# Gate products from two operands, stabiliser rows through memory, and fewer state steps in a one-core encoder layer

## The chip, the cores and the metric

The kernel runs on one core of one Trainium2 chip. The metric is the time of one execution on the device in microseconds (us); lower is better. A core has five engines that matter here: TensorE (PE in the profile, with its weight loads as PEld), VectorE (DVE), ScalarE (ACT), GpSimd (POOL) and SyncE (SP), which only issues DMA transfers in this kernel. Each engine works through its own instructions in the order in which they were written; semaphores hold an instruction back until its inputs are there.

## The reference: what is computed

One encoder layer on x of 2048 tokens by 1024 channels, in float32, between two RMS norms. One input projection gives the operands of two mixers that work side by side: chunked band attention (8 heads of 64) and an mLSTM recurrence (4 heads of 128). Their outputs are gated, summed, projected and added to x; then comes a feed-forward block of width 4096 with a squared ReLU.

The part that the change touches is the recurrence. In the reference:

```python
ig, logf = i_pre, log_sigmoid(f_pre)          # one value per token and head
bcum = cumsum(logf)
dmat = bcum[t] - bcum[s] + ig[s]              # for s <= t, else -inf
m_t  = maximum(bcum + m_state, max_s dmat)    # the stabiliser
dw   = exp(dmat - m_t)
qk   = (q @ k.T) * dw
num  = exp(bcum + m_state - m_t) * (C_state @ q) + qk @ v
den  = exp(bcum + m_state - m_t) * (n_state @ q) + sum(qk)
out  = num / maximum(abs(den), exp(-m_t))
```

The state C, n, m starts at zero and is carried from one chunk of tokens to the next. `i_pre` and `f_pre` are eight columns of the input projection, xn @ w_in: the gates.

## The kernel before

**Blocks.** The 2048 tokens are four blocks (0 to 3) of T = 512, each cut into NT = 4 steps of 128 tokens. A float32 product is made of three single-pass products of split operands: every operand is kept as a high part (rounded, dtype fp32r) and a low part (the rest), and high x high, high x low, low x high are summed (`mm3` at L548 and the loops in `quad`, L597, and `product`, L626). A weight tile of 128x1024 is fetched into one of four `wraw` buffers, then ScalarE rounds it (L489) and VectorE forms its low part (L491) in one of three `wsp` buffers; it serves 24 matmuls.

**Strassen's form.** The large products are run by a two-by-two block scheme with seven products instead of eight. The operand for product m is `A[m][k]`. For the input projection the two rows of blocks are two token blocks, the two columns are the two halves of the 1024 channels: A[0] = a11, A[1] = a12, A[2] = a21 + a22, A[5] = a11 - a21, A[6] = a22, where a11 and a12 are the halves of the first token block (0 or 2), a21 and a22 those of the second (1 or 3).

**The order of the work.** Nothing here is a plain loop. Python generators ("threads", `Flow` at L104) yield requests: `("pe", ns)`, `("act", ns)`, `("dve", ns)`, `("pool", ns)` or `("sp", ns, latency)` with a planned duration, `wait` for events, `get` for buffers. `Flow.run` always takes the request that can start first by these planned times and emits its instructions at once. So the order of each engine's instructions in the program follows from planned durations; on the chip the order is fixed and only the semaphores hold. A changed duration or a dropped instruction places all that comes behind it anew. The dense products (`dense`, L836) form one thread of the lowest rank; all others are put between them.

**Stages.** First the projections of v for blocks 0 and 1 (`token_tiles`), then the input projection of blocks 0 and 1 (`quad`), then that of blocks 2 and 3 (`in_far`, L661) with the mixers of blocks 0 and 1 beside it; then the output projection, the up projection and the down projection (`down`) for blocks 0 and 1, the mixers of blocks 2 and 3 lying beside the last up and the down projection; then the same for blocks 2 and 3, and the final norm. `project(b)` (L920) multiplies the mixers' outputs of block b with their weights; its merges are at L960. It waits until all of them are there (`mixed`).

**The gates.** `gate_mm` (L1373) multiplies the 40 columns of `gw` (eight gate columns, zeros, eight low parts) with `A[m][k]`, eight matmuls of 512 columns a call and pair (m, k0), at L1378. `gates` (L1333) brings the 40 rows to VectorE and transposes them. Block 0: (0,0) and (1,4). Block 1: (0,0), (6,4), and in a second bank (5,0), which is subtracted at L1348. Blocks 2 and 3 share the (0,0) product in `in_far`: it is copied out after the second input group and stored in memory (`gates_kept`, L1366), then (1,4) is added in the same bank for block 2; much later (6,4) and (5,0) follow for block 3, and the stored part is added.

**The stabiliser rows and the head.** `gates_rest` (L1392) turns the gates of a block into all per-token factors; at its end four transposes (L1478) put the stabiliser m_t of the four heads into rows of a bank, and ScalarE (L1480) and VectorE (L1483) keep high and low part in `mtt`. `recurrence` (L1487) runs the four heads of a block one after the other (one place in `rec_room`). Per head, `load_rec` (L1500) writes a column of ones (L1505, GpSimd) and fetches keys, queries (L1509) and values. `rec_head` (L1524) builds exp(dmat - m_t): two matmuls of 512 columns into one bank, the first (L1532) with the causal mask, 0 or -1e30, from bf16 tiles, the second (L1533) with minus m_t of this head copied to all partitions, both over all four steps; four exponentials on ScalarE read the bank (L1537). Then keys are transposed (L1544) and scaled (L1548), k times q is formed (L1555), and each of the four steps has three fp32 products of 129 columns, which take two passes each: with the weights (L1569), the state's update (L1570) and the old state times q (L1571). VectorE updates the state (L1574); `rec_out` (L1622) sums. GpSimd has one power per head (L1591). The recurrence of block b waits for that of block b - 1.

**The norms.** `norm_in` (L976) and `stats_far` (L1003) form 1/sqrt(mean) by a power on GpSimd (L1001, L1023), planned at 960 ns; `rows_far` (L1026) spreads the result by matmuls (L1036). `norm_mid` (L2000) sums squares over partitions with one fp32 matmul of 512 columns against ones (L2012).

## Time and profile before

| what | value |
|---|---|
| median of 3 runs | 2765.6 us (2764.7 to 2769.62) |
| the profiled execution | 2766.63 us |
| its span, first to last instruction | 2764.9 us |
| mean granted TensorE clock | 0.999 |
| DMA moved | 679.28 MB, 246 GB/s in the mean |

The profile is one execution taken by the hardware profiler. Its page gives the busy time of each engine, slices of the span, DMA queues, the chain of work that ended last, and the costliest groups of instructions by line. A group's line reads: line, engine, operation, output<-inputs, shapes, count, then busy time and mean length of one, then idle time of the engine just ahead of them and who ended it. Matmuls overlap in their pipeline, so their lengths add up to more than the time that they take; the distance of their starts is what counts. In the list of waits a row reads: who waited <- for whom, then us in total, times, longest.

### The profile page before, as it was taken

The numbers are of one execution on the slowest core, as the hardware profiler recorded it, in microseconds if no ns is written. First come the engines' busy times: TensorE is split into PE (matmuls) and PEld (weight loads), VectorE is DVE, ScalarE is ACT, GpSimd is POOL, SyncE is SP. The second block draws the span as 40 slices with busy tenths as digits, with TensorE's granted clock in tenths as the row PEclk, the third lists the DMA queues.
The fourth block names the chain that finished last, engine by engine and source line by source line (L and its number), as shares of the span: only waits on it lengthen the run. The fifth ranks groups of instructions, "written<-read, shape, count | busy, mean of one in ns | idle before, by whom it ended". The sixth has DMA issues, their size and how long they took to land.

```text
span 2764.9 us, 38314 instructions
## 1 busy us (share of the span) xinstructions
PE 2733.3 (99%) x12916; PEld 2268.9 (82%) x12916; DVE 2098.3 (76%) x3719; ACT 1552.8 (56%) x2667; POOL 42.2 (2%) x108
## 2 busy tenths in 40 slices
PE   9999999999999999999999999999999999999998
PEld 7878888888888878888888888888888888888887
DVE  7868776787986678997667888788888665667675
ACT  6545456766763435566456776566445555554543
POOL 0000000000000000000000000000000000000000
PEclk9999999999999999999999999999999999999999
DMA  8877678878988899767769876777765464578863
GB/s 280 294 249 269 235 252 268 249 249 274 291 267 271 302 304 313 265 210 264 255 232 295 245 234 213 247 228 226 260 232 172 151 218 152 182 260 279 285 237 115
DMA packets 329704, 679.28 MB, mean 246 GB/s; under 512 B 36692, under 2 KB 62164, under 8 KB 329508
## 3 DMA queue, kind: packets, MB, share of 16 engines
q1 hardware_dynamic: 329364, 676.83, 73.1%
q8 instruction: 101, 1.65, 0.2%
q14 instruction: 95, 0.78, 0.1%
q10 hardware_dynamic: 144, 0.01, 0.0%
HBM read 465.07 MB, written 211.63 MB: 245 GB/s over the span
## 4 chain that ended last, share of the span: by engine, by line
PE 82%; DVE 8%; DMA 3%; issue 3%; ACT 3%; POOL 1%; SPq 0%; POOLq 0%; ACTq 0%; DVEq 0%
PE bank L619 35%; PE bank L551 9%; PE bank L550 9%; PE bank L552 9%; PE bank L650 9%; PE bank L655 2%; PE bank L1216 2%; PE bank L1323 2%; DVE wsp L491 2%; PE bank L1292 2%; DVE r L1080 1%; DMA ctx<-in_xt 1%; DVE sc L1298 1%; ACT wsp L489 1%; PE bank L1378 1%
## 5 line engine op out<-in xcount | busy, mean ns | idle before, releaser
L619 PE MATMUL bank<-r,wsp 128*128 128x512 f32 x4872 | 1113.2, 390 | 3.2 <-DVE ctx L1749 1.6
L619 PEld LDWEIGHTS bank<-r,wsp 128*128 128x128 f32 x4872 | 912.7, 188 | 197.6 <-DVE ctx L1749 2.5
L489 ACT CAST wsp<-wraw 128x1024 fp32r<-128x1024 f32 x453 | 475.7, 1050 | 492.5 <-PE bank L551 172.2
L491 DVE TENSOR_TENSOR wsp<-wraw,wsp 128x1024 fp32r<-128x1024 f32 x453 | 552.7, 1220 | 235.8 <-ACT wsp L489 222.7
L550 PE MATMUL bank<-r,wsp 128*128 128x512 f32 x1152 | 454.5, 395 | 0.0
L551 PE MATMUL bank<-r,wsp 128*128 128x512 f32 x1152 | 449.4, 390 | 0.0
L552 PE MATMUL bank<-r,wsp 128*128 128x512 f32 x1152 | 449.4, 390 | 0.0
L650 PE MATMUL bank<-r,wsp 128*128 128x512 f32 x1512 | 370.7, 393 | 0.8 <-DVE r L1328 0.6
L650 PEld LDWEIGHTS bank<-r,wsp 128*128 128x128 f32 x1512 | 277.5, 188 | 55.0 <-DVE r L1328 1.1
L552 PEld LDWEIGHTS bank<-r,wsp 128*128 128x128 f32 x1152 | 216.3, 188 | 45.9
L551 PEld LDWEIGHTS bank<-r,wsp 128*128 128x128 f32 x1152 | 216.6, 188 | 40.7
L550 PEld LDWEIGHTS bank<-r,wsp 128*128 128x128 f32 x1152 | 216.4, 188 | 40.6
L1080 DVE TENSOR_TENSOR r<-r 128x512 fp32r<-128x512 f32 x271 | 180.3, 686 | 52.5 <-ACT r L1075 51.0
L1075 ACT CAST r<-r 128x512 fp32r<-128x512 f32 x271 | 163.3, 622 | 92.1 <-DMA r<-u 72.6
L1749 DVE TENSOR_TENSOR ctx<-bank,ctx 128x512 f32<-128x512 f32 x150 | 102.5, 685 | 63.3 <-PE bank L619 63.1
L508 DVE TENSOR_TENSOR wraw<-wraw,wraw 128x1024 f32<-128x1024 f32 x112 | 136.2, 1218 | 2.5 <-DMA wsum<-wraw 1.4
L1304 ACT ACTIVATE sc<-sc,scs 128x640 f32<-128x640 f32 (+4 forms) x128 | 97.4, 761 | 50.4 <-DVE scs L1298 49.9
L2067 ACT ACTIVATE ctx<-ctx 128x512 f32<-128x512 f32 x96 | 60.5, 631 | 102.8 <-DVE ctx L1749 102.5
L1741 ACT COPY ctx<-bank 128x512 f32<-128x512 f32 x150 | 87.1, 581 | 50.9 <-PE bank L619 49.9
L1328 DVE TENSOR_TENSOR r<-bank,r 128x512 fp32r<-128x512 f32 (+1 forms) x168 | 96.1, 593 | 16.2 <-ACT r L1326 15.6
L1216 PE MATMUL bank<-r,r 128*128 128x512 f32 x336 | 95.7, 367 | 2.2 <-DVE r L1328 2.2
L1326 ACT CAST r<-bank 128x512 fp32r<-128x512 f32 (+1 forms) x168 | 80.4, 516 | 21.1 <-PE bank L1323 19.6
(248 smaller groups left out, 3014.3 us busy)
## 6 DMA issues: line engine op xcount, KB each, us to landing
wraw<-in_wf SPq DMA_DIRECT2D x202, 512.0 KB, 4.3
wraw<-wsum SPq DMA_DIRECT2D x120, 512.0 KB, 4.8
r<-u SPq DMA_DIRECT2D x224, 256.0 KB, 4.4
u<-ctx SPq DMA_DIRECT2D x128, 256.0 KB, 2.2
u<-tmp SPq DMA_DIRECT2D x96, 256.0 KB, 2.3
wraw<-in_w SPq DMA_DIRECT2D x47, 512.0 KB, 4.2
ctx<-in_wf SPq DMA_DIRECT2D x88, 256.0 KB, 4.0
wsum<-ctx SPq DMA_DIRECT2D x88, 256.0 KB, 3.3
```

Source lines behind the costliest of these rows:

```text
L489: nc.scalar.copy(w[:, 0], raw)
L491: nc.vector.tensor_sub(w[:, 1], raw, w[:, 0].bitcast(F32))
L508: V.tensor_sub(dst, x, y)
L550: mm(ps, lh, rh, start=first, stop=False)
L551: mm(ps, lh, rl, start=False, stop=False)
L552: mm(ps, ll, rh, start=False, stop=last)
L619: mm(ps, wv[:, x, k, n], a[:, y], start=new and k == 0 and x == y == 0, stop=k == 3 and x == 1, skip_group_check=True)
L650: mm(ps, wv[:, x, k, n], a[:, y], start=start and x == y == 0, stop=stop and x == 1, skip_group_check=True)
L1075: self.nc.scalar.copy(dst[:, 0], src)
L1080: self.nc.vector.tensor_sub(dst[:, 1], src, dst[:, 0].bitcast(F32))
L1216: nc.tensor.matmul(bkv[:, :, c0:c0 + w], st, sl[:, :, o:o + w], start=n == 0, stop=n == total - 1)
L1749: nc.vector.tensor_add(t[:, o:o + 512], ps, t[:, o:o + 512])
```

## The change

The change has five parts.

1. **Gates of the second blocks.** `gw` gets four more column groups, the difference of the gate weights of the second and the first half of the channels. Block 1 is then (2,0) and (6,8) in one bank: (a21 + a22) with the first half's weights plus a22 with the difference. Block 2 is (0,0) and (1,4) in one go. For block 3, (2,0) is stored by `gates_kept` when its operand is there, and (6,8) is added to it later. The subtraction L1348, its bank and the event `gclear` go.
2. **Stabiliser rows.** `gates_rest` copies the four rows to a buffer and stores them in memory. `load_rec` fetches one row per head with a load that repeats it on all 128 partitions, into the buffer of the weights, `w`, ahead of keys, queries and values; GpSimd then sets the entries outside the causal triangle to 1e30 in place (`affine_select`, 128x512). The exponentials read `w` with scale -1. The two matmuls L1532 and L1533, the tiles `identb`, `maskb`, `sel`, `nsel`, `mtt` and L1483 go.
3. **Empty state steps.** In block 0, step 0 the product with the old state (which is zero) and its addition are left out. In block 3, step 3 the key's transpose, its scaling and the state's update, which nobody reads, are left out.
4. **The sum in `norm_mid`.** The row of sums is split into high and low part; two single-pass matmuls against ones take the place of the fp32 one. ScalarE's copy and VectorE's subtraction are new.
5. **Planned durations.** The power on GpSimd is planned at 2400 ns in `norm_in` and 5000 in `stats_far`, 960 before. The `temp` buffers are 512 wide, 516 before.

```diff
@@ setup_late
+        nc.vector.tensor_sub(raw[:, 64:96], raw[:, 32:64], raw[:, 0:32])
...
@@ in_far
                     if i == 1:
-                        (gbk,) = yield "get", self.banks, 1
-                        yield from self.gate_mm(gbk, A, ((0, 0),), True, False)
-                        fl.spawn(self.gates_kept(gbk, gclear), 1)
-                    if i == 2:
-                        yield "wait", [gclear]
-                        yield from self.gate_mm(gbk, A, ((1, 4),), False, True)
-                        fl.spawn(self.gates(2, gbk), 1)
+                        (bk,) = yield "get", self.banks, 1
+                        yield from self.gate_mm(bk, A, ((0, 0), (1, 4)), True, True)
+                        fl.spawn(self.gates(2, bk), 1)
...
-                if g == 2 and i == 1:
-                    (one, two) = yield "get", self.banks, 2
-                    yield from self.gate_mm(one, A, ((6, 4),), True, True)
-                    yield from self.gate_mm(two, A, ((5, 0),), True, True)
-                    fl.spawn(self.gates(3, one, two, True), 1)
+                if i == 1:
+                    (bk,) = yield "get", self.banks, 1
+                    yield from self.gate_mm(bk, A, ((2, 0),) if g == 1 else ((6, 8),), True, True)
+                    fl.spawn(self.gates_kept(bk) if g == 1 else self.gates(3, bk, True), 1)
@@ norm_in, stats_far
-        yield "pool", 960
+        yield "pool", 2400
...
-            yield "pool", 960
+            yield "pool", 5000
@@ gates_in
-        for b, use in ((0, (((0, 0), (1, 4)),)), (1, (((0, 0), (6, 4)), ((5, 0),)))):
+        for b, use in ((0, ((0, 0), (1, 4))), (1, ((2, 0), (6, 8)))):
...
@@ gates_rest
-        nc.scalar.copy(self.mtt[:MH], bk[:MH])
-        yield "dve", dve_ns(512)
-        yield "dve", 85
-        V.tensor_sub(self.mtt[32:32 + MH], bk[:MH], self.mtt[:MH].bitcast(F32))
+        nc.scalar.copy(tmp[:MH, :512], bk[:MH])
         fl.put(self.banks, bk)
         fl.set(B["gates"])
+        fl.spawn(self.store(self.mtd.ap()[b], tmp[:MH, :512], B["rows"], self.temp, tmp), 1)
@@ load_rec
         nc.gpsimd.memset(mvv[:, :, 128:129], 1.0)
+        yield "wait", [B["rows"]]
+        yield "sp", 800, 2000
+        nc.sync.dma_start(w[:, :512], self.mtd.ap()[b, h:h + 1].to_broadcast([P, T]))
+        yield "pool", 1000
+        nc.gpsimd.affine_select(out=w[:, :512], in_=w[:, :512], pattern=[[0, NT], [1, P]], compare_op=ALU.is_ge,
+                                fill=-NEG, base=0, channel_multiplier=-1)
+        fl.set(B["row_ev"][h])
         for to, x in ((k, MH + h), (q, h)):
@@ rec_head
-        yield "wait", [B["gates"]]
-        (bk,) = yield "get", self.banks, 1
-        yield "pe", 440
-        mm(bk.rearrange("p (c t) -> p c t", c=NT), self.identb, self.maskb.to_broadcast([P, NT, P]), start=True, stop=False)
-        mm(bk, self.nsel[:, h:h + 1].to_broadcast([P, P]), self.mtt, start=False, stop=True)
+        yield "wait", [B["gates"], B["row_ev"][h]]
...
-            nc.scalar.activation(w[:, c * P:(c + 1) * P], bk[:, c * P:(c + 1) * P], AF.Exp,
+            nc.scalar.activation(w[:, c * P:(c + 1) * P], w[:, c * P:(c + 1) * P], AF.Exp, scale=-1.0,
                                  bias=self.sm["u"][:, n:n + 1])
...
+        kept = NT - 1 if b == NB - 1 else NT
...
+            old = b > 0 or c > 0
...
             mm(bk[:, 0:129], w[:, sl], mv[c], start=True, stop=True)
-            mm(bk[:, 130:259], kt[:, sl], mv[c], start=True, stop=True)
-            mm(bk[:, 260:389], q[:, sl], cst, start=True, stop=True)
+            if c < kept:
+                mm(bk[:, 130:259], kt[:, sl], mv[c], start=True, stop=True)
+            if old:
+                mm(bk[:, 260:389], q[:, sl], cst, start=True, stop=True)
@@ norm_mid
+        nc.scalar.copy(self.part, tot[:, :512])
...
-        nc.tensor.matmul(bk, self.ones[:, 0:1].to_broadcast([P, P]), tot[:, :512], start=True, stop=True)
+        for x in range(2):
+            yield "pe", 227
+            nc.tensor.matmul(bk, self.onesr[:, 0:1].to_broadcast([P, P]), self.part, start=x == 0, stop=x == 1,
+                             skip_group_check=True)
+            if x == 0:
+                yield "dve", dve_ns(512)
+                nc.vector.tensor_sub(self.part, tot[:, :512], self.part.bitcast(F32))
```

89 lines of the change are left out of this document (36 added, 53 removed).

## The prediction

> **What bounds the kernel now.** I read the page's busy line and slices first, then the stages, then the timeline of TensorE.
>
> ```profile
> span 2764.9 us, 38314 instructions
> PE 2733.3 (99%) x12916; PEld 2268.9 (82%) x12916; DVE 2098.3 (76%) x3719; ACT 1552.8 (56%) x2667; POOL 42.2 (2%) x108
> PE   9999999999999999999999999999999999999998
> PEclk9999999999999999999999999999999999999999
> PE 82%; DVE 8%; DMA 3%; issue 3%; ACT 3%; POOL 1%; SPq 0%; POOLq 0%; ACTq 0%; DVEq 0%
> ```
>
> TensorE is busy in 99% of the span, at full clock, in every slice, and holds 82% of the chain of work that ended last. Busy alone proves little, since matmuls overlap; the spacing of their starts decides. From the timeline of TensorE:
>
> ```profile
> 447.62 2.88 PE L619 MATMUL bank<-r,wsp 128*128 128x512 f32 x12
> 450.34 0.39 PE L1532 MATMUL bank<-maskb,identb 128*128 128x512 bf16 x1
> 450.38 0.58 PE L1533 MATMUL bank<-mtt,nsel 128*128 128x512 f32 x1
> 450.80 4.94 PE L619 MATMUL bank<-r,wsp 128*128 128x512 f32 x21
> 455.58 0.60 PE L1544 MATMUL bank<-const,r 128*128 128x128 f32 x4
> 455.94 3.70 PE L619 MATMUL bank<-r,wsp 128*128 128x512 f32 x15
> 459.47 1.05 PE L1555 MATMUL bank<-r 128*128 128x128 f32 x8
> ```
>
> The columns are start, length from first start to last end, line, shapes, count. 21 matmuls of 512 columns take 4.94 us, the last one 0.39 of it, so starts are (4.94 - 0.39)/20 = 0.227 us apart. That is the slot of one matmul, whatever its own 0.39 us says: the queue is full and each slot that goes shortens the stream by 0.227 us. The stages show where this holds (columns: stage, its length, then busy time and count of TensorE, weight loads, DVE, ACT, POOL):
>
> ```profile
> 60.00:400.00 340.00, 337.63 (x1502) 274.88 (x1501) 266.75 (x414) 168.75 (x262) 5.97 (x6) 1.00 0.73 259
> 500.00:600.00 100.00, 96.48 (x532) 80.80 (x532) 79.12 (x235) 68.06 (x163) 5.50 (x17) 1.00 0.74 229
> 700.00:800.00 100.00, 98.52 (x540) 84.04 (x540) 88.07 (x213) 70.71 (x150) 3.25 (x11) 1.00 0.88 281
> 1700.00:1800.00 100.00, 97.97 (x532) 82.78 (x531) 76.65 (x180) 58.17 (x134) 3.72 (x8) 1.00 0.77 239
> 1900.00:2700.00 800.00, 799.17 (x3577) 661.81 (x3576) 578.03 (x795) 424.49 (x632) 3.23 (x4) 1.00 0.64 221
> ```
>
> Even where the mixers (attention and recurrence) run beside the dense products, TensorE is idle only 1.5 to 3.5 us in 100. So the end is set by the sum of TensorE's slots, plus about 30 us of gaps.
>
> **The change, part by part.** First what TensorE loses.
>
> ```profile
> L1378 PE MATMUL bank<-r,gw 128*40 128x512 f32 x72 | 18.1, 395 | 0.0
> L1532 PE MATMUL bank<-maskb,identb 128*128 128x512 bf16 x16 | 6.2, 389 | 0.0
> 464.46 0.39 PE L1569 MATMUL bank<-ctx,ctx 128*128 128x129 f32 x2
> 464.69 0.39 PE L1570 MATMUL bank<-ctx,ctx 128*128 128x129 f32 x2
> 464.91 0.39 PE L1571 MATMUL bank<-cst,r 128*128 128x129 f32 x2
> 465.05 1.64 PE L650 MATMUL bank<-r,wsp 128*128 128x512 f32 x6
> 466.52 0.39 PE L1569 MATMUL bank<-ctx,ctx 128*128 128x129 f32 x2
> 1300.86 1.02 PE L2012 MATMUL bank<-bias,ones 128*128 128x512 f32 x2
> 1301.32 4.92 PE L619 MATMUL bank<-r,wsp 128*128 128x512 f32 x19
> ```
>
> 1. Gates. Block 1 took 24 matmuls, with the difference weights 16; blocks 2 and 3 together take 32 before (8 for a product that both use, 8 more for block 2, 16 more for block 3) and 32 after (16 and 8 + 8). 72 become 64: 8 x 0.227 = 1.8 us.
> 2. Mask and stabiliser row. 16 heads lose the pair L1532 and L1533; the pair stands between starts at 450.34 and 450.80, that is 0.46 us: 16 x 0.46 = 7.3 us.
> 3. Empty state. A step of the recurrence has three fp32 products (two passes each). From 464.46 to 466.52 are 2.06 us with six slots of L650 (1.36), so the three cost 0.70, one 0.233 us. In block 0, step 0, four heads leave out the product with the state: 4 x 0.233 = 0.9 us. In block 3, step 3, four heads leave out the state update, 0.233, and one transpose: from 455.58 to 459.47 are 3.89 us with fifteen slots (3.40), so four transposes cost 0.48, one 0.12. 4 x 0.353 = 1.4 us.
> 4. The row sum in norm_mid. One fp32 product becomes two single-pass products. The nineteen L619 behind it end their last start 5.22 us after 1300.86 (1301.32 + 4.92 - 0.39 + 0.227 - 1300.86 = 5.22), of which 19 x 0.227 = 4.31 are theirs: the old one costs 0.91, the new two 0.45. 4 x 0.45 = 1.8 us.
>
> Sum: 1.8 + 7.3 + 0.9 + 1.4 + 1.8 = **13.2 us** of TensorE's stream.
>
> Second, the planner's allowance for the power on GpSimd rises from 960 ns to 2400 (norm_in) and 5000 (stats_far). The trace shows why it matters:
>
> ```profile
> PE bank L1036 <- POOL r_in L1001: 2.5, 2, 1.2
> PE bank L1036 <- POOL r_in L1023: 1.8, 1, 1.8
> 197.05 1.01 POOL L1023 TENSOR_TENSOR r_in<-r_in,half 128x4 f32<-128x4 f32 x1 [145.72 <-DVE r_in L1021]
> 249.70 4.38 POOL L1023 TENSOR_TENSOR r_in<-r_in,half 128x4 f32<-128x4 f32 x1 [51.65 <-DVE r_in L1021]
> 49.39 1.94 POOL L1001 TENSOR_TENSOR r_in<-r_in,half 128x4 f32<-128x4 f32 x1 [18.63 <-DVE r_in L997]
> 71.01 6.06 DMA ctx<-in_xt
> 249.54 0.74 DVE L1656 SCALAR_TENSOR_TENSOR tmp<-tmp,gcol,bias 128x512 f32<-128x512 f32 x1
> 252.00 1.22 DVE L491 TENSOR_TENSOR wsp<-wraw,wsp 128x1024 fp32r<-128x1024 f32 x1
> ```
>
> TensorE idles 4.3 us in all because L1036 was placed before GpSimd was done. A later place lets other products go first. I count the 1.8 us (the stage at 250 is dense) and not the 2.5: the later of those two powers starts at 49.39, and up to 77 us the chain of work that ended last still runs over loads of x, so products moved forward there would only wait for those. Bounds 0 and 4.3. Total **15 us**.
>
> Third, what is added and what hides it. Per block the rows are stored (one issue) and per head fetched by a 256 KB broadcast load; SP issues 20 more. In this trace such loads land in 4.1 us (r<-mfar), and SP already stands in line without TensorE feeling it:
>
> ```profile
> r<-mfar SPq DMA_DIRECT2D x32, 256.0 KB, 4.1
> SPq L451 <- DVE wsp L491: 299.3, 152, 8.1
> ```
>
> The new row load waits on SP until the store has landed, some 4 us, in front of weight loads and u loads; single waits of up to 8.1 us stand in that queue now (152 of them for L451), covered by the four raw weight tiles, one per 24 slots or 5.4 us. I cost it at nothing; without that cover it is 4 x 4 = 16 us. For the first head the keys and queries are now issued behind the row, not ahead of it.
>
> The masked select on GpSimd over 128x512 has no row in this trace. From below: a memset of 64 columns takes 146 ns and one of 4 takes 109, which is 0.6 ns a column and 0.42 us for 512. From above: 4.4 us, the longest GpSimd row. I take 1.0 us, the usual power row, the nearest one that reads SBUF. The Trainium skill, "GPSIMD Engine Reference", section 3.1, has about 1.8 cycles per element for a tight loop and about 12 with data-dependent branching; at its 1.2 GHz that is an estimate of 0.8 or 5.1 us, and no run here shows either. By the first the sum stays at 15 us; by the second the blocking described below would cost 16 x 5.1 / 2 = 41 us and the time be 2792.
>
> So per head row load plus select, 4.1 + 1.0, stand ahead of the exponentials, and in each block the store some 4 more. Keys are issued about 4 us later than now. Behind the waiting select on GpSimd stand only bias memsets and the power of the head before; behind the exponentials on ACT stand the casts of weights. The block grows by about 9 + 4 x 3 = 21 us. What waits for it is the projection:
>
> ```profile
> 1667.98 0.69 DVE L1607 TENSOR_TENSOR ctx<-bank,tmp 128x512 f32<-128x512 f32 x1
> 1724.35 0.68 DVE L960 SCALAR_TENSOR_TENSOR tmp<-tmp,bank 128x512 f32<-128x512 f32 x1
> ```
>
> Block 2, the tightest, ends its recurrence at 1668.7 and its projection first merges at 1724.35: 56 us of cover for 21. Past 56 each microsecond would count fully.
>
> ACT and DVE gain a little: four L1483 (0.68), two L1348 (0.67) and eight small ones go, four splits in norm_mid come (0.69 on DVE, 0.62 on ACT); they are off the path by the stages above, and I cost them at nothing.
>
> The profiled execution took 2766.63 us around its span of 2764.9; the median is 2765.6. 15 off the median gives **2751 us**.
>
> **The rivals.**
>
> A wait takes the removed slots' place. ACT is in order, and the plan allows 3.8 us for row load and select where I expect 5.1.
>
> ```profile
> ACT r L1075 <- DMA r<-u: 72.6, 73, 4.2
> ACT ctx L1537 <- PE bank L1533: 10.2, 5, 5.5
> ```
>
> ACT now waits about 1 us at each late u load, and it once waited 5.5 us at the exponentials, without a gap of that size on TensorE. For it: ACT is 58 to 71% busy there, and the casts feed TensorE. Against it: three split weight tiles are 16 us of cover. If TensorE loses 0.5 us per head, 16 x 0.5 = 8 are given back: 2759.
>
> GpSimd and DVE block each other; this one ends slower. The power at 249.70 took 4.38 us while DVE ran two-input operations without a pause from 249.54 to 253.2, and 1.01 us beside an idle DVE at 197.05: the two exclude each other, and the select reads 128 times as many columns. If it takes 4.4 us and holds DVE for it, DVE loses 16 x 4.4 = 70 us in the mixer stages, where it is 77 to 88% busy and makes the low halves of the weights (L491). Two selects per 100 us are 8.8 us; at 700 to 800 only 12 are free. It decides from about 6 us a select in the mean, or earlier where two fall behind one another; with half of the 70 landing on TensorE the time is 2751 + 35 = 2786. Against it: in this trace it is GpSimd that waits, DVE's lengths stay as they are (1.22 at 252.00).
> The Trainium skill, "SBUF — State Buffer", section "Who interferes with whom", says that a DVE instruction with two SBUF inputs and a GpSimd instruction that reads SBUF share a read interface, and whichever starts first blocks the other for its whole length. The trace agrees for GpSimd behind DVE (4.38 against 1.01); DVE behind GpSimd isn't shown in it.
>
> The change gives more: all of the 4.3 us, and a new order closes a few of the 15 us of gaps in the mixer stages: 2745.
>
> The rebuilt order loses what the slots give. The planner places every instruction anew, and gaps of 1 to 2 us appear elsewhere; eight of 1.5 us make 2763. That the slots don't go at all is excluded: their instructions are gone.
>
> **How the numbers follow.** Forecast 0.62 (2746 to 2757); wait in the removed slots' place 0.15 (2759, 2756 to 2763); order loses it 0.06 (2763); more 0.07 (2745); blocking 0.10 (2786). About 0.2% (5.5 us) is what a measurement of this kernel can tell from no change, so faster means under 2760.1 and slower over 2771.1. Faster: 0.62 + 0.07 + two thirds of 0.15 + 0.02 = 0.81. Slower: 0.10. Same: 0.09. The range reaches from the better case to the order's loss, 2743 to 2763; outside are the blocking and a tenth.
>
> **What would show it.** TensorE's matmul count falls by 8 for the gates, 32 for mask and row, 8 and 12 for the empty steps (two passes a product, one a transpose), and 0 in norm_mid, 60 in all, and its busy time by about 13 us, at idle near 30. The select's row gives its length, and beside it L491's mean tells whether DVE was held (1220 ns now). The waits of ACT's exponentials on GpSimd tell the first rival: over 30 us in all would bear it out. L1036 should wait for GpSimd no more. The prediction is wrong if idle of TensorE in 400 to 900 and 1480 to 1900 grows by more than 5 us.

## The result and the profile after

The kernel after takes 2759.52 us (median of 8 runs, 2756.09 to 2762.49), the kernel before, beside it on the same chip, 2766.97 us (8 runs, 2761.78 to 2772.07). The ratio is 0.9973, 95% interval 0.9962 to 0.9984: 7.5 us faster, where the sum said 15. The direction was right, the size about half. The page of the kernel after, its profiled execution taking 2758.38 us:

```profile
span 2756.6 us, 38227 instructions
...
PE 2725.7 (99%) x12856; PEld 2265.7 (82%) x12856; DVE 2098.2 (76%) x3715; ACT 1551.2 (56%) x2665; POOL 50.4 (2%) x124
```

TensorE has 60 instructions fewer, as forecast, but its busy time fell by 7.6 us, not by 13, and its idle time stayed (2756.6 - 2725.7 = 30.9 against 31.6). So 5.6 us of the forecast loss of busy time are missing. Three stretches of 3.41 us each, in which TensorE was granted half its clock, hold 5.1 of them, since work at half clock counts as busy (see Theory C). The same stages as before the change, and one more (1100 to 1200), with the columns of the prediction; the number after the five engines is the granted clock:

```profile
60.00:400.00 340.00, 339.99 (x1515) 278.14 (x1515) 265.56 (x410) 171.38 (x265) 3.73 (x8) 1.00 0.75 265
500.00:600.00 100.00, 95.44 (x521) 79.16 (x520) 80.06 (x225) 69.46 (x166) 6.92 (x17) 1.00 0.82 249
700.00:800.00 100.00, 97.96 (x538) 82.96 (x537) 81.23 (x202) 69.36 (x156) 4.69 (x14) 0.98 0.88 289
1100.00:1200.00 100.00, 98.16 (x424) 80.02 (x423) 91.40 (x125) 57.03 (x85) 0.00 (x0) 0.98 0.64 220
1700.00:1800.00 100.00, 97.40 (x506) 81.94 (x507) 76.24 (x193) 54.07 (x117) 4.65 (x10) 0.98 0.75 240
1900.00:2700.00 800.00, 797.27 (x3571) 660.23 (x3570) 578.50 (x805) 425.59 (x637) 3.23 (x4) 1.00 0.63 219
```

The first stage lost its gap (337.63 busy before, 339.99 now: the wait of the row spread is gone). Three stages show a clock of 0.98, which the profile before never had there. What the prediction named as its tests, first the groups by line of GpSimd, of ScalarE and of VectorE:

```profile
L1488 POOL TENSOR_SCALAR_AFFINE_SELECT ctx<-ctx 128x512 f32<-128x512 f32 x16 | 11.4, 713 | 103.7 <-DMA ctx<-mrow 103.3 <-ACT ctx L1529 0.3
```

```profile
L1518 ACT ACTIVATE ctx<-ctx,g_u 128x128 f32<-128x128 f32 x64 | 22.2, 394 | 3.3 <-POOL ctx L1488 3.3
```

```profile
L482 DVE TENSOR_TENSOR wsp<-wraw,wsp 128x1024 fp32r<-128x1024 f32 x453 | 553.4, 1222 | 223.6 <-ACT wsp L480 215.4
```

Then the row's load in the list of transfers (count, KB each, us from issue to landing; 4.1 was assumed), and TensorE's longest rows in the list of waits:

```profile
ctx<-mrow SPq DMA_DIRECT2D x16, 256.0 KB, 5.3
```

```profile
PE bank L1308 <- ACT sc L1296: 4.1, 4, 2.6
PE bank L1277 <- DVE scs L1283: 3.0, 3, 1.2
PE bank L1201 <- DVE r L1313: 2.5, 2, 1.3
PE bank L1021 <- POOL r_in L986: 1.5, 2, 1.0
```

The select takes 0.71 us (1.0 was assumed, between 0.42 and 4.4). The exponentials wait 3.3 us in all for it; over 30 would have borne out the first rival. VectorE's low halves take 1222 ns where they took 1220, 0.9 us more over all 453, so the second rival's blocking isn't there to speak of. The row spread (L1021 now) still waits 1.5 us, of 4.3. The first three waits of TensorE stood in the profile before too, at 2.5, 0.3 and 2.2 us, and have grown. All three end links of the attention: its transposes (L1308) wait for the softmax's normalisation (L1296), its scores (L1277) for the row minima that free the banks (L1283), its products (L1201) for the split transposes (L1313).

**Where along the kernel.** The dense matmuls are 10560 in every kernel here. The start of the k-th in one trace less that in another tells how much has been gained up to there. Worked out from the traces, in us, each column what was gained or lost within a stretch (the stretch between 302 and 393 changes nothing):

```
stretch, starts in before (us)      5-302  393-898   898-1454  1454-1980  1980-2752   sum
dense matmuls                      0-1200 1600-3200 3200-5600  5600-7200  7200-10559
beside them                               mixers0,1           mixers2,3
due by the prediction                -3.6     -2.8      -2.7      -5.1       -0.9   -15.1
after less before                    -6.4     +1.0      +0.4      -1.9       -1.5    -8.4
```

(Due in the second stretch: eight pairs 3.65 and four empty steps 0.93 go, eight gate slots of the moved (2,0) come.) The start gave more than was due (2.4 of its 6.4 us by 123 us, where profiles of the same order differ by about 2); both mixer stages, and the dense stretch between them, gave little or nothing: 3.8, 3.1 and 3.2 us less than was due. In each of these three stands one place with new waits of TensorE, 1.8 to 2.6 us, and 3.41 us at half clock behind them (at 750, 1128 and 1701 us; shown under Theory C).

### The profile page after: what moved, and what is told of

It reads as the page before. It is cut to its first block, busy times and chain, and to the rows that moved or that the text cites. A ratio compares the mean times of both kernels' runs of the same rounds, so it can differ in the third digit from the quotient of the medians.

```text
span 2756.6 us, 38227 instructions
## 1 busy us (share of the span) xinstructions
PE 2725.7 (99%) x12856; PEld 2265.7 (82%) x12856; DVE 2098.2 (76%) x3715; ACT 1551.2 (56%) x2665; POOL 50.4 (2%) x124
## 3 DMA queue, kind: packets, MB, share of 16 engines
q8 instruction: 101, 1.65, 0.2%
## 4 chain that ended last, share of the span: by engine, by line
PE 88%; DVE 5%; issue 2%; ACT 2%; DMA 2%; POOL 0%; SPq 0%; POOLq 0%; ACTq 0%; DVEq 0%
PE bank L610 38%; PE bank L541 10%; PE bank L542 10%; PE bank L543 10%; PE bank L641 10%; PE bank L646 2%; PE bank L1201 2%; PE bank L1277 2%; PE bank L1308 2%; DVE wsp L482 1%; ACT wsp L480 1%; PE bank L1551 0%; ACT sc L1289 0%; DVE r L1065 0%; DMA r<-qfar 0%
## 5 line engine op out<-in xcount | busy, mean ns | idle before, releaser
L482 DVE TENSOR_TENSOR wsp<-wraw,wsp 128x1024 fp32r<-128x1024 f32 x453 | 553.4, 1222 | 223.6 <-ACT wsp L480 215.4
L1313 DVE TENSOR_TENSOR r<-bank,r 128x512 fp32r<-128x512 f32 (+1 forms) x168 | 96.5, 593 | 10.2 <-ACT r L1311 9.3
L1201 PE MATMUL bank<-r,r 128*128 128x512 f32 x336 | 97.5, 373 | 2.8 <-DVE r L1313 2.5
```

The costliest lines, as they stand in the source:

```text
L482: nc.vector.tensor_sub(w[:, 1], raw, w[:, 0].bitcast(F32))
L1201: nc.tensor.matmul(bkv[:, :, c0:c0 + w], st, sl[:, :, o:o + w], start=n == 0, stop=n == total - 1)
```

## The experiments

The theories. **A**: each slot that goes from TensorE lands, and the order that the planner makes anew takes the rest back. **B**: in the mixer stages TensorE isn't the only bound, so slots removed there turn into waits for VectorE and ScalarE. **C**: the loss is the stretches at a lower clock. **D**: the row's path (store, load, select) costs in itself. Later came **E** (VectorE plays no part) and **F** (the length of the attention's chain, whichever engine a link is on, is what TensorE meets). All ratios are to runs of the kernel before on the same chip, with 95% intervals.

### The removed work with the plan of before

In `fixed_order` the planner still counts the removed work, so that every engine should keep the order of before. The exponentials read a buffer that GpSimd fills with zeros:

```diff
 (rec_head)
-        mm(bk.rearrange("p (c t) -> p c t", c=NT), self.identb, self.maskb.to_broadcast([P, NT, P]), start=True, stop=False)
-        mm(bk, self.nsel[:, h:h + 1].to_broadcast([P, P]), self.mtt, start=False, stop=True)
 ...
 (load_rec)
+        nc.gpsimd.memset(B["ctx"][h][3][:, :512], 0.0)
 ...
 (gate_mm, block 1's product (5,0))
+                if skip:
+                    continue
 ... (and the state steps that the change leaves out)
```

> The planner is told nothing: every planned duration of the kernel before stays, so each engine keeps its order, and only instructions go: the 8 gate products and the subtraction of block 1, the pair of mask and row in 16 heads, the state products that the change leaves out. Left out of the computation: block 1's third gate product, mask and stabiliser (the exponentials take constants, from a buffer that GpSimd fills with zeros). norm_mid and the planned powers stay as before. Theory A, the removed slots land one for one and the changed kernel lost some 5 to 6 us to its new order: 11.4 us faster than before (1.8 + 7.3 + 0.9 + 1.4), ratio 0.9959. Theory B, TensorE isn't the bound in the mixer stages and slots that go there are given back to other waits: only the 1.8 us of the gates and some 2 more, ratio about 0.9985. Theory C, what is lost is lost to windows of half clock that the gaps bring on: the spread over runs goes with the granted clock, some 2 us for each 0.001 of it.

Measured: 2767.96 us, 0.9985 (0.9976 to 0.9994), 4.2 us. Of 11.4 us only a third arrives. But the run doesn't have quite the order that it was meant to keep: planned durations alone don't settle the order, and in its trace some tens of instructions stand a few places from where they stood before; why isn't known. Up to 750 us the removed slots land, head by head: by the starts of the dense matmuls the trace is ahead of the one before by 1.5 us at 450, 3.2 at 525, 4.1 at 600, 5.0 at 690 and 5.5 at 750, which is 4.0 of the 4.6 us due in this stage. At 766 us it is ahead by 2.0. What lies between stands in the timeline of TensorE (start, length, line, operation, count, and in brackets the idle time ahead and who ended it), below it that of VectorE, and last that of VectorE in the kernel before at the same place:

```profile
757.22 0.41 PE L1577 MATMUL bank<-cst,r 128*128 128x129 f32 x2
759.33 2.54 PE L650 MATMUL bank<-r,wsp 128*128 128x512 f32 x6 [1.70 <-DVE ctx L754]
761.67 1.05 PE L1216 MATMUL bank<-r,r 128*128 128x512 f32 x2
```

```profile
756.15 0.67 DVE L1229 TENSOR_TENSOR tmp<-bank,tmp 64x512 f32<-64x512 f32 x1
756.75 0.33 DVE L1581 SCALAR_TENSOR_TENSOR cst<-cst,g_ex,bank 128x129 f32<-128x129 f32 x1
757.01 0.41 DVE L1234 TENSOR_TENSOR tmp<-tmp 64x256 f32<-64x256 f32 x1
757.45 1.23 DVE L491 TENSOR_TENSOR wsp<-wraw,wsp 128x1024 fp32r<-128x1024 f32 x1
758.59 0.68 DVE L754 TENSOR_TENSOR ctx<-bank,ctx 128x512 f32<-128x512 f32 x1
```

```profile
761.14 0.67 DVE L1229 TENSOR_TENSOR tmp<-bank,tmp 64x512 f32<-64x512 f32 x1
761.75 0.67 DVE L754 TENSOR_TENSOR ctx<-bank,ctx 128x512 f32<-128x512 f32 x1
...
762.93 1.21 DVE L491 TENSOR_TENSOR wsp<-wraw,wsp 128x1024 fp32r<-128x1024 f32 x1
```

VectorE has no pause, and TensorE stands 1.70 us until a bank is evacuated at 759.3 by L754. In the kernel before, L754 stands ahead of L491, here behind it, which puts it off by about the length of the wait (L1234 and L491 together take from 757.01 to 758.59). The six matmuls behind take 2.54 us where six took 1.55 elsewhere: (2.54 - 0.39)/5 = 0.43 us apart, which is twice the slot. The records of the granted clock have half speed from 759.8 for 3.41 us. The wait and the half clock (1.7 us) are the 3.5 us. The waits for the attention ahead of this place didn't grow: 1.17, 1.39 and 0.99 us at 478, 546 and 577 us, and 1.17, 1.40 and 0.99 at the same matmuls before; one of 0.61 at 691 came, one of 0.65 went. So the run doesn't tell A from B: slots land where the order is kept, and the largest loss goes with an order that isn't. The other losses of its trace (1.7 us between 898 and 1454, where nothing was removed, and 3.3 missing behind 1454) have no cause shown.

`fixed_order_row` puts the row's path back, planned at no time at all, so that nothing leads it:

```diff
+            fl.spawn(self.load_row(b, h), 1)      # row load and select as in the change, planned at 0 ns
```

> As fixed_order, but with the row path: the block's rows are stored, and per head the row is loaded to all partitions and masked by GpSimd, put into the order with a planned duration of zero, so that nothing else moves. Left out: block 1's third gate product, and the low half of the stabiliser. Theory A (the new order is what costs): the row path itself costs nothing to 1 us, ratio 0.996 like fixed_order. Theory D (the row path costs: a wait of ACT's exponentials on load and select, or SP standing at the store): some 5 us less gain than fixed_order, ratio about 0.998, and ACT's exponentials wait more than 20 us for GpSimd. In this kernel the row is fetched only when the block's stabiliser is there, with no lead planned, so its waits are an upper bound.

Measured: 2768.36 us, 0.9997 (0.9987 to 1.0007), some 3 us over `fixed_order` (the intervals overlap). The expectation's "so that nothing else moves" wasn't met either: most of what lies between the dense matmuls stands at another place in its trace. The exponentials wait 8.9 us for the select, where Theory D expected over 20. TensorE's longest wait, 4.30 us at 756, is for the load of the values, which SP issues behind eight loads of another tensor, and half clock follows for 6.83 us. So the 3 us can't be put down to the row alone. In the kernel after, which plans 3.8 us for it, the exponentials' 3.3 us of waits are all that shows of it: Theory D isn't borne out.

### The planned durations, and an order for its own sake

`powers_only` is part 5 of the change alone; `other_order` changes two other planned durations by a little, no work:

```diff
 powers_only: norm_in, stats_far
-        yield "pool", 960
+        yield "pool", 2400
-            yield "pool", 960
+            yield "pool", 5000
 other_order: the power per head, the bias memset
-        yield "pool", 960
+        yield "pool", 1010
-        yield "pool", 180
+        yield "pool", 290
```

> The kernel before with the planned durations of the power on GpSimd alone changed, to 2400 and 5000 ns: no instruction comes or goes, only the order. The prediction counted 1.8 us of gain (bounds 0 and 4.3); the trace of the changed kernel shows its first 300 us 4.6 us shorter in gaps. Expected 1.8 to 4.6 us faster, ratio 0.9983 to 0.9993, and TensorE's wait of L1036 for GpSimd gone, if a new order does no harm elsewhere; under theory A a new order moves the time by several us of either sign beside that.

> The kernel before with two planned durations set to what the trace has, 960 to 1010 ns for the head's power and 180 to 290 for the two bias memsets; both engines' work is the same, instruction for instruction, only the order in the mixer stages differs. Theory A: the time moves by 2 to 6 us, of either sign, without any work changed; that is the size of what an order is worth. Theories B and D: within 1.5 us of before.

Measured: `powers_only` 2767.28 us, 0.9987 (0.9978 to 0.9996), 3.6 us, as expected, with 2.9 us of the waits of L1036 left at the first place; `other_order` 2772.79 us, 1.0005 (0.9996 to 1.0014). This new order by itself costs 1.4 us (a gain of 1.1 to a loss of 3.9). That is one order; what the order of the change costs isn't bounded by it, and Theory A stays open. The plan for the power is by its median worth half of the whole change (1.1 to 6.1 us). Its place in the kernel after, from the timeline:

```profile
244.66 4.01 PE L610 MATMUL bank<-r,wsp 128*128 128x512 f32 x17
248.51 1.05 PE L1021 MATMUL bank<-const,r_in 128*128 128x128 f32 x8
249.32 12.97 PE L610 MATMUL bank<-r,wsp 128*128 128x512 f32 x56
```

Before, the same matmuls stood at 254.14 after 1.80 us of waiting; now nothing waits. The dense matmuls gain 2.07 us there in the trace of `powers_only`. The power itself also got shorter at its new place, 1.38 us here and 1.01 in `powers_only` against 4.38 before, so the later place of L1036 isn't the only reason why the wait went.

### The parts alone

`rows_only` is part 2 on the kernel before. `parts_345` is parts 3, 4 and 5 on it. The expectation of `parts_345` speaks of new gate products too; that is a mistake in its text, since the kernel kept the gates of before, so its numbers are 1.8 us (0.0007) too low for what ran: 0.9973 by A and 0.9980 by B.

```diff
 rows_only (load_rec, rec_head)
+        nc.sync.dma_start(w[:, :512], self.mtd.ap()[b, h:h + 1].to_broadcast([P, T]))
+        nc.gpsimd.affine_select(out=w[:, :512], in_=w[:, :512], pattern=[[0, NT], [1, P]], ...)
-        mm(...identb, maskb...)
-        mm(...nsel, mtt...)
 parts_345 (rec_head, norm_mid, norm_in, stats_far as in the change)
```

> Part 2 of the change alone, in the order that the planner makes of it: rows stored, broadcast load and select on GpSimd, mask and row pair gone from TensorE (7.3 us of slots), nothing else. Theory A (slots land): 0.9973. Theory B (slots of the mixer stages are not what ends them): 0.9985 to 1.0005, 1 to 2 us of gain at most, with an order that may move it by 1.5 us. Theory D (the row path costs in itself): over 1.0005.

> The change without parts 1 and 2 as they touch block 1 and the heads: gates of all blocks from two operands and their new order, norm_mid's row sum in two single passes, the power's planned 2400 and 5000 ns, and the empty state steps left out; the mask and row pair stays. Theory A: 13.2 less 7.3 slots plus 3.6 for the power, or 9.5 us, 0.9966, with all of the change at 0.994. Theory B: the parts that lie in dense stages (gates 1.8, norm_mid 1.8, power 3.6) land, 7.2 us, 0.9974, and so as much as the whole change gives (0.9973); part 2 then adds nothing.

Measured: `rows_only` 2768.68 us, 0.9990 (0.9981 to 0.9998), 2.8 us; `parts_345` 2763.79 us, 0.9975 (0.9965 to 0.9985), 6.9 us. Of the 2.8 us of `rows_only` the trace has 2.07 at the row spread near 250 us, where its new order happens to place L1036 later, so the pair's 7.3 us of slots are worth about 0.7 (the interval of the run is 0.6 to 5.3). The part with the largest sum gave the least. Its trace has two waits that the kernel before doesn't have, 2.20 us at 750 and 2.61 at 1707, and half clock at 1608 and 1710. `parts_345` doesn't tell A from B.

### The mirror: more work on TensorE

`pair_twice` issues the pair a second time, with the plan of before:

```diff
         mm(...identb, maskb...)
         mm(...nsel, mtt...)
+        mm(...identb, maskb...)
+        mm(...nsel, mtt...)
```

> The kernel before, in its own order, with the mask and row pair issued twice for every head (the second time over the first): 16 x 0.46 = 7.3 us more of TensorE's slots in the mixer stages, nothing else. Theory A (each slot there lengthens the stream): 1.0026. Theory B (VectorE is as late as TensorE there, so TensorE has slack): a third to a half lands, 2 to 4 us, 1.0008 to 1.0014.

Measured: 2777.56 us, 1.0035 (1.0022 to 1.0048), 6 to 13 us longer for 7.3 us of slots. So Theory B as it was put, with slack for TensorE, misses: work added lands in full (+4.7 and +3.8 us in the two mixer stages of its trace, 3.65 due in each; +2.1 more at 254, where a half-speed window follows the wait for the power). Like the slots removed in `fixed_order` up to 750 us, the added ones move the stream by their own size.

### What the other bound is

Three kinds of relief, each applied to `before` and to `fixed_order`, all with the planned durations of before; the difference in each pair is what the same removed slots are worth under it. In-place operations are left out, and the planner still counts them:

```diff
 light_dve, 177 us of VectorE: sum_w, conv_far (two), rec_head, the attention's fold, scores
-                V.tensor_sub(dst, x, y)
+                if n == 4:
+                    V.tensor_sub(dst, x, y)
-            nc.vector.scalar_tensor_tensor(d5, z[:, n:n + 512], cw[:, n:n + 1], d5, op0=ALU.mult, op1=ALU.add)
-        nc.vector.scalar_tensor_tensor(d5, z[:, :512], 1.0, d5, op0=ALU.add, op1=ALU.mult)
-        V.tensor_mul(ndv[:, :, :128], ndv[:, :, :128],
-        nc.vector.tensor_add(tmp[own, :256], tmp[own, :256], tmp[own, 256:512])
-            nc.vector.tensor_scalar(e[:, :n], e[:, :n], st[:, 3:4], None, op0=ALU.mult)
 light_act, 81 us of ScalarE: scores, conv_far
-            nc.scalar.mul(e[:, :n], e[:, :n], st[:, 3:4])
-        nc.scalar.activation(z[:, :512], d5, AF.Tanh, scale=0.5)
 no_norm, 61 us of ScalarE and 24 of VectorE: scores
-            nc.vector.tensor_scalar(e[:, :n], e[:, :n], st[:, 3:4], None, op0=ALU.mult)
-            nc.scalar.mul(e[:, :n], e[:, :n], st[:, 3:4])
```

> The kernel before, in its own order, with six kinds of in-place VectorE operations left out of the stages where mixers run (the weight differences of sum_w, the three taps and the last product of the convolution, the division of the recurrence's output, the fold of the attention's output, and VectorE's share of the softmax's normalisation; the planner still counts them). All of TensorE's work stays. It is the partner of fixed_order_light_dve. Theory B (in the mixer stages VectorE and the attention's chains are as late as TensorE): before, TensorE waits only some 5 us in all for VectorE and ScalarE in those stages, so little can be won: ratio 0.997 to 1.000. Theory E (VectorE plays no part): 1.000.

> fixed_order (TensorE loses the third gate product of block 1, the mask and row pair and the empty state steps, 11.4 us by the slots, at the order of before) with the same VectorE operations left out as in before_light_dve. What counts is the difference to before_light_dve: without that relief fixed_order gained only 0.0015 (4 us). Theory B, with VectorE as the engine that is late next: the removed slots now land, the difference is 9 to 11 us (0.0032 to 0.0040). Theory E (the slots are lost to something else, to the half-clock windows by themselves, to ScalarE, to the DMA queues): the difference stays at 3 to 5 us (0.001 to 0.002).

> The kernel before, in its own order, with two kinds of in-place ScalarE operations left out: ScalarE's share of the softmax's normalisation (79, 0.77 us each, on the attention's chain) and the tanh of the convolution (32, 0.63 us), 81 us of ScalarE in all. The partner of fixed_order_light_act. Theory B (VectorE as such is late): ScalarE is 56% busy, little to be won, 0.998 to 1.000. Theory F (the attention's chain is late, whichever engine): as with VectorE's relief, 0.995 to 0.997.

> fixed_order (11.4 us of TensorE's slots left out: third gate product of block 1, mask and row pair, empty state steps) with the same ScalarE operations left out as in before_light_act. What counts is the difference to before_light_act. Theory B: 3 to 5 us, as without relief (0.001 to 0.002). Theory F: the slots land, 9 to 11 us (0.0032 to 0.0040).

> The kernel before, in its own order, with the softmax's normalisation left out altogether (79 on ScalarE, 61 us; 49 on VectorE, 24 us): one link of the chain scores, exponential, reciprocal, normalisation, transposes; all else stays. The partner of fixed_order_no_norm. Theory F (the chain's length decides): TensorE's 5 to 6 us of waits for these two lines (5.8 us at the transposes) and the gaps behind them go, 0.996 to 0.998. Theory B (VectorE's room decides): 24 of 177 us of relief, 0.998 to 1.000.

> fixed_order (11.4 us of TensorE's slots left out) with the normalisation left out as in before_no_norm. What counts is the difference to before_no_norm. Theory F: the slots land, 8 to 11 us (0.0029 to 0.0040). Theory B: VectorE is hardly relieved, 3 to 6 us (0.0011 to 0.0022).

Measured (differences of ratios times 2767 us, with the two intervals combined):

```
relief      before                       fixed_order                  the removed slots give
none        1                            0.9985 (0.9976 to 0.9994)     4.2 +- 2.5 us
light_dve   0.9964 (0.9950 to 0.9977)    0.9926 (0.9914 to 0.9939)    10.5 +- 5
light_act   0.9981 (0.9973 to 0.9990)    0.9956 (0.9944 to 0.9968)     6.9 +- 4
no_norm     0.9980 (0.9972 to 0.9989)    0.9949 (0.9937 to 0.9962)     8.6 +- 4
```

Each relief lets more of the 11.4 us land, and `no_norm`, which takes one link of 0.5 to 0.8 us out of the chain and little of an engine's time, as much as the others: its expectation under F (8 to 11) is met and that under B (3 to 6) lies at the lower end of its interval. By these times alone none of the three is apart from the unrelieved 4.2. Misses on the way: `light_act` lands between its two expectations (3 to 5 and 9 to 11); of the partners, `before_light_act` met Theory B (0.998 to 1.000) and not F (0.995 to 0.997), and `before_light_dve` gained a little more than B allowed (0.997). The traces add the place (fixed_order less its partner, in the stretches of above):

```
                 5-302  393-898   898-1454  1454-1980  1980-2752   sum
slots removed     -1.8     -4.6       0         -5.1        0     -11.4
none              -1.5     +0.1     +1.7        -1.8      -0.2     -1.7
light_dve         -0.6     -3.6     -1.0        +1.7      +2.5     -1.0
light_act         -3.6     -3.8     -0.9        -6.6      +1.1    -13.9
no_norm           -2.1     -4.3     +1.6        -3.7      +3.1     -5.4
```

In the first mixer stage the slots land under every relief (3.6 to 4.3 of 4.6) and not without (0.1 the wrong way). That difference is the one place at 757 us: in both kernels of every relieved pair L754 stands ahead of L491, and neither the wait nor the half clock is there. Without its 3.5 us the row `none` would have -3.4 in this stage, like the others. (The two traces of that row are also from different measurements: the kernel before takes 2767.0 us beside the kernel after and 2770.7 beside `fixed_order`.) One profile per kernel is noisy elsewhere: a half-speed window at 1859 in the relieved `fixed_order` of the second row, and one at 2574 in the last, move single cells by 2 to 3 us. The stage from 700 to 800, first of `fixed_order`, then of `fixed_order_no_norm`:

```profile
700.00:800.00 100.00, 97.07 (x521) 82.29 (x520) 84.92 (x208) 67.38 (x142) 3.76 (x12) 0.98 0.86 274
```

```profile
700.00:800.00 100.00, 99.76 (x550) 85.93 (x549) 83.38 (x205) 65.14 (x139) 3.82 (x12) 1.00 0.89 284
```

550 matmuls instead of 521 in the same 100 us, at full clock, with VectorE as busy as it was (83.38 and 84.92): VectorE's share of busy time isn't what changed. The wait at 757 and the half clock behind it are about 15 of the 29 matmuls. The waits of TensorE from 400 to 900 in `fixed_order`:

```profile
PE bank L1323 <- ACT sc L1311: 2.7, 5, 1.0
PE bank L1323 <- DVE sc L1309: 2.3, 3, 1.4
PE bank L650 <- DVE ctx L754: 1.7, 1, 1.7
PE bank L1216 <- DVE r L1328: 1.7, 2, 1.2
```

The first two are the link that `no_norm` takes out, on ScalarE and on VectorE alike. In the kernel before they stood at 2.5 and 1.7: with 4.6 us of slots removed they grew by 0.8. So Theory F isn't shown: a shorter chain saves waits, but it isn't what took the removed slots in the first mixer stage of `fixed_order`. For the second stage the runs settle nothing.

`pair_twice_light_dve` and `after_light_dve` put the same VectorE relief on `pair_twice` and on the kernel after (no new edit).

> pair_twice with the VectorE operations left out as in before_light_dve (0.9964). With VectorE relieved Theory B has TensorE as the only bound, so the pair lands nearly in full: 6 to 8 us over before_light_dve, 0.9986 to 0.9993. If the difference is as small as without the relief (2 to 4 us, 0.9971 to 0.9978), VectorE isn't what gave the slack.

> The kernel after, in its own order, with the same kinds of VectorE operations left out as in before_light_dve (weight differences, taps and last product of the convolution, division of the recurrence's output, fold of the attention's output, VectorE's share of the normalisation). Theory B: with VectorE relieved the change is worth what its slots and its power say, 13 to 16 us against before_light_dve: 0.9906 to 0.9917. Theory A (the new order, not VectorE, costs the rest): it is worth what it is worth without relief, 7.5 us: 0.9937.

Measured: `pair_twice_light_dve` 2763.4 us, 0.9981 (0.9972 to 0.9989), 4.7 +- 4.4 us over its partner, between the two expectations and no help. `after_light_dve` 2745.76 us, 0.9922 (0.9909 to 0.9935), 11.6 +- 5 us under its partner: towards the 13 to 16 of B, and 7.5 not excluded.

### Moving work instead of leaving it out

Three versions of the kernel after with all of its work, each taking work from VectorE in a mixer stage:

```diff
 after_pool_sums (sum_w, the sixteen in the first mixer stage)
-                V.tensor_sub(dst, x, y)
+                self.nc.gpsimd.tensor_tensor(dst, x, y, op=ALU.subtract)
 after_sums_later
-SUMS.update({... enumerate(((1, 4), (1, 8), *((4, i) ...
+SUMS.update({... enumerate(((2, 3), (2, 8), *((4, i) ...
 after_norm_act (scores)
-        e0 = yield "act|dve", 60 + dve2_ns(n)
+        e0 = yield "act", act_ns(n, ap=1)
```

> The kernel after with the sixteen weight differences of sum_w that fall in the first mixer stage (128x512 each, 0.683 us on VectorE) computed by GpSimd instead, planned at 2 us each; nothing is left out. Theory B: VectorE has 11 us more room in a stage where it is late, which is worth 2 to 4 us: 0.9960 to 0.9966 against 0.9973 for the kernel after. Rival from the prediction (GpSimd and VectorE block each other over a read of 128x512): 16 subtractions of two SBUF operands hold VectorE or are held by it, nothing is won, and the time is that of after or up to 10 us over it, 0.9973 to 1.001.

> The kernel after with the two weight differences of sum_w that start in the first mixer stage (16 subtractions, 11 us of VectorE, and 16 loads and 16 stores) started a stage later, after the mixers of blocks 0 and 1; nothing is left out. Theory B: VectorE has room where it is late, 2 to 5 us off the kernel after: 0.9955 to 0.9966. Theory F or A: no more than a new order does, 0.9968 to 0.9978.

> The kernel after with the softmax's normalisation always on ScalarE, where the planner now chooses (54 of 128 on VectorE, 0.49 us each): VectorE loses 27 us in the mixer stages, ScalarE gains 42; nothing is left out. Theory B: VectorE is what is late, ScalarE has room: 0.995 to 0.9966. Theory F: the chain gets longer by 0.3 us for each of the 54 and ScalarE fuller, no gain or a loss: 0.9973 to 1.000.

Measured: 2765.97 us, 0.9984 (0.9976 to 0.9993); 2766.88 us, 0.9988 (0.9978 to 0.9998); 2765.02 us, 0.9984 (0.9976 to 0.9993). None beats the kernel after (0.9973); all three are some 3 to 4 us worse, at the edge of the intervals. The loss of `after_norm_act` is what F expected and B didn't, but its trace has it elsewhere than in the chain: in the first mixer stage it loses 8.4 us against the kernel before, where a wait of 4.33 us for the load of keys ends at 749.6 and half clock follows for 6.83 us. `after_sums_later` removes 11 us of VectorE's time from the stage for nothing and misses every expectation; its trace has new waits too, the longest 2.72 us at 757. All three have an order of their own, so they decide neither between B and F nor against A. In `after_pool_sums` the relief was none, as GpSimd's and VectorE's timelines show:

```profile
551.99 3.17 POOL L425 TENSOR_TENSOR ctx<-ctx,ctx 128x512 f32<-128x512 f32 x2 [1.07 <-DMA ctx<-in_wf]
...
558.23 3.50 POOL L425 TENSOR_TENSOR ctx<-ctx,ctx 128x512 f32<-128x512 f32 x2 [3.07 <-DMA wsum<-ctx]
```

```profile
549.90 1.23 DVE L486 TENSOR_TENSOR wsp<-wraw,wsp 128x1024 fp32r<-128x1024 f32 x1
...
552.60 1.40 DVE L1223 TENSOR_TENSOR tmp<-tmp 64x256 f32<-64x256 f32 x1
...
558.47 2.11 DVE L486 TENSOR_TENSOR wsp<-wraw,wsp 128x1024 fp32r<-128x1024 f32 x1 [0.59 <-ACT wsp L484]
```

L486 takes 1.23 us alone and 2.11 when it starts behind a GpSimd subtraction; L1223 1.40 where its mean is 0.44. In these two places a subtraction (1.41 us in the mean on GpSimd) holds VectorE for 0.9 to 1.0 us, longer than the 0.68 us that VectorE takes for it.

### The stretches at half clock (Theory C)

The timeline of TensorE in the kernel after, at the place where the stage from 700 to 800 lost its clock, then the stage table over 749 to 760, then the timeline at the other two places:

```profile
750.77 0.56 PE L1277 MATMUL bank<-r,r 128*128 128x320 f32 x2 [0.51 <-DVE scs L1283]
752.58 1.30 PE L1277 MATMUL bank<-r,r 128*128 128x320 f32 x4 [1.25 <-DVE scs L1283]
753.89 3.40 PE L641 MATMUL bank<-r,wsp 128*128 128x512 f32 x9
```

```profile
749.00:752.70 3.70, 1.94 (x13) 1.42 (x12) 3.70 (x12) 2.19 (x5) 0.11 (x1) 1.00 1.04 371
752.80:756.20 3.40, 3.39 (x10) 2.51 (x10) 3.40 (x14) 3.30 (x7) 0.00 (x0) 0.50 0.94 319
756.30:760.00 3.70, 3.70 (x23) 3.15 (x22) 2.43 (x11) 2.67 (x9) 0.00 (x0) 1.00 0.87 301
```

```profile
1128.88 1.20 PE L610 MATMUL bank<-r,wsp 128*128 128x512 f32 x4 [0.63 <-DVE r L1067]
1131.29 8.94 PE L610 MATMUL bank<-r,wsp 128*128 128x512 f32 x31 [1.20 <-DVE ctx L1944]
```

```profile
1703.73 0.56 PE L1308 MATMUL bank<-const,sc 128*128 128x128 f32 x3 [2.60 <-ACT sc L1296]
...
1707.64 0.63 PE L542 MATMUL bank<-r,wsp 128*128 128x512 f32 x1
1708.07 0.59 PE L543 MATMUL bank<-r,wsp 128*128 128x512 f32 x1
1708.49 0.40 PE L541 MATMUL bank<-r,wsp 128*128 128x512 f32 x1
1708.73 0.40 PE L542 MATMUL bank<-r,wsp 128*128 128x512 f32 x1
```

In 3.7 us with two gaps TensorE was busy 1.94; then it runs 3.4 us at half clock, 10 matmuls where the next 3.7 us have 23. At 1708 starts are 0.43 us apart and, from 1708.49, 0.24. The kernel after has three such windows (752.8, 1131.6 and 1705.1, each 3.41 us), each worth 3.41/2 = 1.7 us. A window between 750 and 762 is in six of the seven profiles in which the pair is gone without relief, in none of the nine in which the pair stays, and in none of the four with the pair gone and relief.

Each window of the kernel after follows waits of TensorE (0.51 and 1.25 us, 0.63 and 1.20, 2.60), so Theory C is no cause of its own: the windows make new waits dearer. Two of the three places go with the planner's order. The waits of 0.63 to 0.65 and 1.20 to 1.21 us near 1130 stand in the kernel after and in its three versions with all the work, and in no kernel with the planned durations of before; the wait of 2.60 us near 1705 stands in the kernel after, `after_pool_sums`, `after_sums_later` and `rows_only`, while the same link never waits longer than 1.5 us in a kernel that plans the pair. Nor are they all waits for the attention: those near 1130 are for VectorE outside the mixers, where it was busy without a pause. This speaks for Theory A's second half, a new order that loses what the slots give; no run isolates it.

Not every such wait brings a window: the same two near 1130 did in the kernel after and in `after_sums_later`, and didn't in `after_norm_act` and `after_pool_sums`. Over all runs the granted clock is 0.9975 in the mean for the kernel after, 0.9984 for the kernel before beside the other runs and 0.9982 for `fixed_order`. As an estimate, 0.0009 of 2760 us is 2.5 us, a third of the 7.5 that are missing; for `fixed_order` it is 0.6.

## Why the prediction was half right

- **The step that failed** is the end of "So the end is set by the sum of TensorE's slots, plus about 30 us of gaps", with the "full clock, in every slice" of the profile before taken over. The price of a slot held: the eight gate slots land (the trace of `fixed_order` gains 1.9 us where they were), the pairs land head by head up to 750 us, and the pair issued twice costs its slots in full. The sum put at nothing what the planner's new order makes TensorE wait for, and what the clock does behind such a wait. In the kernel after, idle time is 30.9 us as forecast, but 6.2 of them are new waits at three places (750, 1128 and 1701 us), in place of others that went; behind each the clock was half for 3.41 us, 5.1 us in all, and busy time fell by 7.6 us where 13 were counted. That these waits come from the order is argued from the traces, where two of them recur with the same lengths in other kernels with a changed plan, and in none with the plan of before. `fixed_order` was to isolate it, and loses most where its own order differs. So the cause stays in part open.
- **The reading of the stage table.** Idle time of 1.5 to 3.5 us in 100 was taken to mean that nothing else was late. Small idle on a saturated engine says that the others keep up with it in that order, not by how much: one evacuation two instructions later on VectorE cost 3.5 us at 757.
- **The term for L1036** came out: 1.8 us counted, 3.6 measured (1.1 to 6.1), 2.07 in the traces at its place. Of the 4.3 us of waits 1.5 remain, all in the first of the two places, as the prediction had it in kind.
- **Norm_mid, gates and the empty steps as counts** were right: 60 instructions fewer, and norm_mid's term lands (dense matmuls gain 1.2 us in the stretch behind the mixers of blocks 2 and 3, 0.9 due).
- **The rivals.** "A wait takes the removed slots' place" had the time, 2759, by luck, and the wrong wait: row and select cost the exponentials 3.3 us in all. The blocking didn't come: the select was 0.71 us. It is a real mechanism, as `after_pool_sums` shows, for two-operand work of twice that length. "The rebuilt order loses what the slots give", gaps of 1 to 2 us elsewhere, was given a chance of 0.06 and describes best what the trace of the kernel after shows, three such places instead of eight.
- **The test that was blind.** "Wrong if idle of TensorE grows by more than 5 us" in the mixer stages: it didn't grow. The loss hid in matmuls at half clock, which count as busy, and in new waits that stand in for old ones. The comparison of starts of equal matmuls shows it, busy time doesn't.

What stays open: whether the slots would land in full in an order that is kept exactly; what `fixed_order` loses between 898 and 1454 us and in the second mixer stage; and whether the parts add up (2.8 + 6.9 + 1.9 = 11.6 us against 7.5 +- 3).

## What to carry to other kernels

A removed instruction of a saturated engine can be priced at its slot only while the order of everything else stays; where a planner places the rest anew, put a term for new waits beside the sum. Judge afterwards by the starts of the same instructions in both traces, not by busy time: the places where the gain is lost show at once, and the granted clock there says how much of it is the clock. Before a run "with the plan of before" is used as proof, compare the order of the instructions in the two traces. A planned duration that is too short at one wait was worth 3.6 us here (1.1 to 6.1), beside 4.2 (1.7 to 6.7) for all the work removed in `fixed_order`.

## What the hardware showed unexpectedly

- Gaps of 0.5 and 1.25 us, or one of 2.6 us, were followed by 3.41 us at half the clock; one of 1.80 us at 254 in the kernel before wasn't, and gaps of the same lengths near 1130 were in two kernels and weren't in two others. The Trainium skill, "TensorE: Matmul & The Clock Gate", Part 1, gives a free-running window of 3413 ns and half rate after at least one idle window. The length agrees; the trace differs in that no window was idle: in the 3.41 us before each of the three, TensorE was busy for 1.65, 1.57 and 1.37 us.
- GpSimd's subtraction of two 128x512 operands took 1.41 us, and VectorE's two-operand instructions beside it grew from 1.23 to 2.11 us. The Trainium skill, "SBUF — State Buffer", "Who interferes with whom", says that the one that starts first blocks the other; the prediction saw that for GpSimd behind VectorE only, and this run shows it for VectorE behind GpSimd.
- The masked select of 128x512 took 0.64 us in 13 of 16 cases (0.71 in the mean), less than the power over 4 columns (1.0 us).
